# A hybrid mixer block on one core: the emission planner prices every operation, and TensorE keeps the planner's order

## The chip, the core and the metric

The kernel runs on one core of a Trainium2 chip. The core has TensorE (PE, matmuls into PSUM), VectorE (DVE), ScalarE (ACT), GpSimd (POOL) and SyncE (SP, which issues the DMAs here). Each engine runs its own instructions in the order in which they stand, and waits on semaphores for the others. The metric is the device time of one execution in microseconds (us); less is better.

## What is computed

One layer: RMS norm of x (2048 tokens by 1024), one input projection, four mixers of 256 channels each, one output projection, a second RMS norm and the residual.

```python
h = _rmsnorm(x, pre_norm_w[l])
proj = jnp.einsum('btd,de->bte', h, w_in[l])
p_gdn, p_rwkv, p_sc, p_gla = _split(proj, [GDN_COLS, RWKV_COLS, SC_COLS, GLA_COLS])
y_gdn = _gated_deltanet(p_gdn, ...)   # conv, chunks of 64, triangular solve per chunk, scan over chunks
y_rwkv = _rwkv7(p_rwkv, ...)          # token shift, decays, a recurrence over tokens (chunked in the kernel)
y_sc = _short_conv(p_sc, ...)
y_gla = _gla(p_gla, ...)              # gated linear attention, scan over chunks
out = jnp.einsum('bte,ed->btd', jnp.concatenate([y_gdn, y_rwkv, y_sc, y_gla], -1), w_out[l])
x = x + _rmsnorm(out, post_norm_w[l])
```

## The kernel before

**Tiling.** The tokens go in four blocks of 512. The projection of a block is made of large matmuls: 128 rows of weights by 512 tokens, in three passes (the high and low parts of the activations, tiles `hh` and `hl`, and of the weights, tiles `w`), into PSUM tile `pp`, of which there are two. A step of `proj` is four large matmuls (two where two tiles are woven), then a `yield`. The output projection at the end (tiles `woh`, `wol`) has the same form. In all there are 3808 large matmuls among 8180.

**Small work.** Per block and per pair of 128 tokens there is an inverse of eight unit-triangular matrices for the delta rule and again for RWKV (`inverse`: sixteen in all). A level of it is: `psi<-X,Bb` on TensorE, a VectorE multiply into `W` (line 591), `psi<-W,Yb` on TensorE, a VectorE add into `X` (line 596), a transpose and two copies into `Y` and `Yb`. The chains (`gdn_chain`, `rwkv_chain`, `gla`) carry the states `Sg`, `Sr`, `Sl` from chunk to chunk: for RWKV a loop is `psc<-Sr,AR` on TensorE, a ScalarE copy into `ru`, `psc<-ru,Yf`, a VectorE multiply into `UV`, `psc<-UV,BK`, and the addition to `Sr`. `gdn_prep`, `gdn_mats`, `gdn_more`, `rwkv_prep`, `rwkv_mats` and `rwkv_more` make what these need. Their matmuls and transposes go into `psa`, of which there are three tiles, each one PSUM bank; `psi` has one and `psc` two.

**What sets the order.** Each kind of work is a generator (a thread with a priority): chains 0, inverses 1, `prepare` 2, the outputs 3, statistics of the next block 4, loads of the output weights 5, and the large matmuls of `projections` 99. `weave` lets them take turns while the program is emitted. It keeps a running time `self.t`, to which only matmuls add (`mm`, `tr`); a thread that yields a number is ready again that much later, and the numbers are constants in `LAT` (for example 1.0 us from the matmul of an inverse's level to the next). The large matmuls go on until small work is ready and `BEAT` = 1.5 us have passed since the last. Then a list scheduler below the kernel takes the emitted program and orders each engine's instructions by its own estimate of what is ready, with the place of emission as priority; `high_priority` moves loads and evictions forward. So TensorE's order in the program is the scheduler's: of its instructions, 1946 stand behind one that was emitted later. A projection tile's group in `projections` waits for events, among them `("R", blk - 1)`: the RWKV tiles of a block may be overwritten when the block before has been put out.

Of the kernel before, what the change touches and what calls it, by code (L numbers as in the profile page):

```python
# [125 lines left out]
class Ring:  # L126
# [6 lines left out]
    def __call__(self):  # L133
# [15 lines left out]
    "lqk": (BL, 2), "lv": (BL, 2), "lkv": (384, 1), "lgz": (2 * BL, 1), "ld": (8, 1), "lg": (BL, 2), "n32": (32, 4), "gs": (TT, 2),  # L149
# [17 lines left out]
BEAT = 1.5  # L167
# [3 lines left out]
LAT = {"gates": 6.0, "ipre": 2.0, "gates2": 1.0, "norms": 3.2, "chan": 0.9, "pool": 1.38, "decay": 2.6, "mats": 2.2, "more": 1.4, "inv0": 1.0, "inv1": 2.2,  # L171
       "invr": 0.8, "chA": 1.0, "chB": 0.7, "chC": 0.48, "rpre": 5.0, "rchan": 4.5, "gpre": 3.0, "gA": 1.1,
       "gB": 0.62, "out": 8.0, "front": 0.3, "rdec": 0.6, "fdone": 2.0, "wo0": 2.8, "wo1": 1.4, "bonus": 2.5}
# [14 lines left out]
class K:  # L188
    def __init__(self, tc, a, out):
        self.tc, self.nc, self.a, self.out = tc, tc.nc, a, out  # L190
        self.t, self.left, self.ev, self.threads = 0.0, 0.0, {}, []


    def mm(self, out, w, x, **kw):
        n = math.prod(out.shape[1:])
        self.t += max(0.028, n * (1.67e-3 if w.dtype == F32 else 0.42e-3))
        return self.nc.tensor.matmul(out, w, x, **kw)  # L197

    def tr(self, out, x, ident):
        self.t += out.shape[1] * 0.83e-3  # L200
        return self.nc.tensor.transpose(out, x, ident)  # L201
# [5 lines left out]
    def done(self, *ev, lat=0.0):  # L207
        self.ev[ev] = self.t + lat
# [8 lines left out]
    def step(self, th):  # L217

        y = next(th[3], "end")
        if y == "end":  # L220
            self.threads.remove(th)
        elif isinstance(y, tuple):
            th[2] = y
        else:
            th[1] = self.t + y

    def weave(self):
# [3 lines left out]
        while self.threads:  # L231
# [10 lines left out]
            else:  # L242
                if not any(self.can(th) for th in self.threads):
                    w = [th[1] for th in self.threads if th[2] is None]
                    assert w, [(th[0], th[2]) for th in self.threads]
                    self.t = max(self.t, min(w))


    def setup(self, ctx):
# [16 lines left out]
        def bank(name, n):  # L266
            p = E(tc.tile_pool(name=name, bufs=n, space=PSUM))
            return lambda: p.tile([P, 512], F32, name=name, tag=name)
# [101 lines left out]
    def stats(self, blk, keep=None):  # L370
# [4 lines left out]
        ss, x, r = self.small(2 * TT), self.small(TT), self.R["gs"]()  # L375
# [29 lines left out]
    def front(self, blk, r):  # L405
# [3 lines left out]
        if blk:  # L409
            yield "bonus", blk - 1  # L410
        ps = self.psa()
# [9 lines left out]
        for k in range(KT):  # L421
# [12 lines left out]
            if k % 2:  # L434
                self.done("F", blk, k // 2, lat=LAT["fdone"])
            yield LAT["front"]
# [39 lines left out]
    def proj(self, blk, groups):  # L476
# [14 lines left out]
        for n, j, i, ks in work:  # L491
# [24 lines left out]
            if last:  # L516
                with self.tc.high_priority(offset=PRIO):
                    tiles[j][1](ps)
                if j + 1 == len(tiles) and after:
                    self.done("P", blk, after, lat=2.5)  # L520
# [37 lines left out]
    def inverse(self, Bh, Bl, n):  # L558
# [27 lines left out]
        yield LAT["ipre"]  # L586
        for lv in range(4):
# [4 lines left out]
            yield LAT["inv0"]  # L592
# [7 lines left out]
            yield LAT["inv0"] if lv == 3 else LAT["inv1"]  # L600
# [4 lines left out]
        yield LAT["inv0"]  # L605
# [13 lines left out]
        yield LAT["invr"]  # L619
# [8 lines left out]
        yield LAT["inv0"]  # L628
# [50 lines left out]
    def gates_prep(self):  # L679
# [31 lines left out]
        yield LAT["gates"]  # L711
# [16 lines left out]
        yield LAT["gates2"]  # L728

    def gdn_prep(self):  # L730
# [8 lines left out]
        for tt in range(TT):  # L739
# [11 lines left out]
            yield LAT["chan"]  # L751
# [16 lines left out]
        yield LAT["norms"]  # L768

    def gdn_mats(self, tt, Bh, Bl):  # L770
# [10 lines left out]
        yield LAT["pool"]  # L781
# [5 lines left out]
        yield LAT["decay"]  # L787
# [67 lines left out]
    def rwkv_prep(self, blk):  # L855
# [10 lines left out]
        for pr in range(2):  # L866
# [30 lines left out]
            yield LAT["rpre"]  # L897
# [18 lines left out]
        yield LAT["rchan"]  # L916

    def rwkv_bonus(self, blk):

        nc = self.nc  # L920
        for pr in range(2):
            v, gz, add = self.r["v"][pr], self.r["gz"][:, pr, :], self.r["add"][:, pr, :]
            self.split(*self.S, add)
            yield LAT["bonus"]
# [35 lines left out]
    def rwkv_more(self, tt, m):  # L960
# [8 lines left out]
        yield LAT["rdec"]  # L969
# [16 lines left out]
    def gdn_chain(self, tt, m, Y):  # L986
# [5 lines left out]
        for cp in range(2):  # L992
# [10 lines left out]
            yield LAT["chA"]  # L1003
# [6 lines left out]
            yield LAT["chB"]  # L1010
# [4 lines left out]
            if cp == 0:  # L1015
                yield LAT["chC"]
# [15 lines left out]
    def rwkv_chain(self, tt, m, Y):  # L1032
# [11 lines left out]
        for cp in range(2):  # L1044
# [6 lines left out]
            yield LAT["chB"]  # L1051
# [7 lines left out]
            yield LAT["chB"]  # L1059
# [4 lines left out]
            if cp == 0:  # L1064
                yield LAT["chC"]
# [58 lines left out]
    def prepare(self):  # L1124

        n = 0
        for blk in range(NBLK):
            for name in "GR":
# [8 lines left out]
                for pair in range(TT // 2):  # L1137
# [12 lines left out]
                    self.done("B", n, lat=LAT["mats"])  # L1150
# [4 lines left out]
                    self.done("M", n, lat=LAT["more"])  # L1155
# [3 lines left out]
            self.done("Lprep", blk, lat=LAT["gpre"])  # L1159

    def inverses(self):
        for n in range(NBLK * TT):
# [4 lines left out]
            self.done("I", n, lat=LAT["inv0"])  # L1167

    def chains(self):

        n = 0
        for blk in range(NBLK):
            for name, chain, norm, out in (("G", self.gdn_chain, self.gdn_norm, self.gdn_out),
                                           ("R", self.rwkv_chain, self.rwkv_norm, self.rwkv_out)):
                for tt in range(TT):
# [14 lines left out]
                    yield LAT["chC"]  # L1190
# [5 lines left out]
    def put(self, name, blk, tt, o, out):  # L1196
        if name == "R":
            yield "bonus", blk
        yield LAT["out"]
# [72 lines left out]
    def gla(self, blk, tt):  # L1272
# [15 lines left out]
        yield LAT["gA"]  # L1288
# [11 lines left out]
        for cp in range(2):  # L1300
# [4 lines left out]
            if cp == 0:  # L1305
                yield LAT["gB"]
# [7 lines left out]
        yield LAT["gB"]  # L1314
# [18 lines left out]
    def load_out(self):  # L1333
# [3 lines left out]
        for i in range(2):  # L1337
            for c in range(KT):
# [3 lines left out]
                yield LAT[f"wo{i}"]  # L1342
            self.done("W", i, lat=2.0)
# [114 lines left out]
```

## Time and profile before

| | us |
|---|---|
| three runs, median (lowest to highest) | 1389.66 (1388.5 to 1394.49) |
| the profiled execution, its own time | 1384.26 |
| its span, first to last instruction | 1382.4 |
| TensorE busy (9928 matmul records) | 1283.9, 93% |
| TensorE's weight loads busy | 976.0, 71% |
| VectorE busy | 955.6, 69% |
| ScalarE busy | 529.4, 38% |
| GpSimd busy | 355.0, 26% |

Busy times are shares of the span. A matmul's record is longer than the time until the next one starts, because matmuls are pipelined; so where the text prices TensorE it goes from start to start. A matmul of 32-bit floats has two records, a transpose or another type has one.

### The profile page before, as it was taken

The numbers are of one execution on the slowest core, as the hardware profiler recorded it, in microseconds if no ns is written. First come the engines' busy times: TensorE is split into PE (matmuls) and PEld (weight loads), VectorE is DVE, ScalarE is ACT, GpSimd is POOL, SyncE is SP. The second block draws the span as 40 slices with busy tenths as digits, with TensorE's granted clock in tenths as the row PEclk, the third lists the DMA queues.
The fourth block names the chain that finished last, engine by engine and source line by source line (L and its number), as shares of the span: only waits on it lengthen the run. The fifth ranks groups of instructions, "written<-read, shape, count | busy, mean of one in ns | idle before, by whom it ended". The sixth has DMA issues, their size and how long they took to land.

```text
span 1382.4 us, 25708 instructions
## 1 busy us (share of the span) xinstructions
PE 1283.9 (93%) x9928; PEld 976.0 (71%) x9928; DVE 955.6 (69%) x2194; ACT 529.4 (38%) x1181; POOL 355.0 (26%) x437
## 2 busy tenths in 40 slices
PE   5979878999989999999999898999998998999997
PEld 3757656777767667767777676677776766778886
DVE  5766798786765898777676996776769866533322
ACT  4653444333822441335523432345224333332221
POOL 5554343330120221111211211111211143333221
PEclk9999998999999999999999999999999999999999
DMA  7866442544534323354543333543444254334442
GB/s 269 278 230 229 164 171 92 176 147 165 176 112 152 117 97 125 112 183 142 167 155 129 116 104 111 173 144 112 145 141 134 83 170 138 111 104 145 146 151 99
DMA packets 98506, 204.47 MB, mean 148 GB/s; under 512 B 9152, under 2 KB 39248, under 8 KB 98384
## 3 DMA queue, kind: packets, MB, share of 16 engines
q1 hardware_dynamic: 98384, 202.83, 44.4%
q8 instruction: 78, 1.28, 0.4%
q14 instruction: 44, 0.36, 0.1%
HBM read 153.51 MB, written 49.28 MB: 147 GB/s over the span
## 4 chain that ended last, share of the span: by engine, by line
PE 52%; DVE 18%; issue 4%; POOL 3%; ACT 3%; DMA 2%; SPq 0%; POOLq 0%; ACTq 0%; DVEq 0%
PE pp L197 39%; PE psc L197 6%; PE psa L197 3%; PE psi L197 2%; PE psa L201 2%; POOL sm L354 2%; DVE Yb L583 1%; DMA x<-in_xt 1%; DVE X L596 1%; DVE W L591 1%; DVE Y L598 1%; DVE t L879 0%; DVE AR L895 0%; DVE M L949 0%; DVE og L1023 0%
## 5 line engine op out<-in xcount | busy, mean ns | idle before, releaser
L197 PE MATMUL pp<-hh,w 128*128 128x512 f32 (+1 forms) x2272 | 646.0, 408 | 5.3 <-DMA w<-parts 3.2
L197 PEld LDWEIGHTS pp<-hh,w 128*128 128x128 f32 (+1 forms) x2272 | 412.0, 190 | 90.6 <-DMA w<-parts 4.1
L197 PE MATMUL pp<-hl,w 128*128 128x512 f32 (+1 forms) x1152 | 342.7, 410 | 2.0 <-POOL hl L433 2.0
L197 PEld LDWEIGHTS pp<-hl,w 128*128 128x128 f32 (+1 forms) x1152 | 210.8, 191 | 47.7 <-POOL hl L433 3.8
L350 POOL TENSOR_TENSOR w<-raw,w 128x512 fp32r<-128x512 f32 (+1 forms) x102 | 129.4, 1270 | 218.0 <-ACT w L349 105.1
L349 ACT CAST w<-raw 128x512 fp32r<-128x512 f32 (+1 forms) x102 | 60.3, 593 | 141.9 <-issue 74.5
L354 POOL TENSOR_TENSOR sm<-sm,mhalf 128x4 f32<-128x4 f32 (+1 forms) x64 | 59.0, 922 | 209.2 <-DVE sm L1091 185.5
L659 DVE SCALAR_TENSOR_TENSOR pq<-pq,par,pq 128x512 f32<-128x512 f32 x72 | 59.1, 821 | 17.1 <-ACT pq L656 14.5
L197 PE MATMUL pp<-woh,w 128*128 128x512 f32 x256 | 69.5, 395 | 0.0
L197 PEld LDWEIGHTS <-Yb 128*128 128x128 f16 x640 | 26.0, 100 | 43.1 <-issue 18.8
L197 PE MATMUL psi<-W,Yb 128*128 128x64 f16 x640 | 33.6, 197 | 24.2 <-DVE W L591 20.8
L833 ACT COPY pq<-pp 128x512 f32<-128x512 f32 x36 | 21.1, 587 | 90.6 <-PE pp L197 90.6
L583 DVE COPY Yb<-Y 64x512 f16<-64x512 f16 x160 | 53.7, 336 | 2.1
L197 PEld LDWEIGHTS <-Bb 128*128 128x128 f16 x768 | 31.0, 99 | 33.8 <-issue 30.2
L197 PEld LDWEIGHTS pp<-woh,w 128*128 128x128 f32 x256 | 47.2, 188 | 9.5
L596 DVE TENSOR_TENSOR X<-psi,X 128x512 f16<-128x512 f32 x64 | 43.9, 686 | 13.3 <-PE psi L197 12.9
L197 PE MATMUL psi<-X,Bb 128*128 128x64 f16 x768 | 40.1, 197 | 12.9 <-DVE X L579 9.3
L591 DVE TENSOR_TENSOR W<-psi,c 128x512 f16<-128x512 f32 x64 | 44.0, 688 | 9.3 <-PE psi L197 8.3
L1391 DVE SCALAR_TENSOR_TENSOR pq<-pq,sm,x 128x512 f32<-128x512 f32 x32 | 25.1, 784 | 33.9 <-DMA x<-in_x 23.2
L598 DVE STREAM_TRANSPOSE Y<-X 128x512 f16<-128x512 f16 x64 | 45.1, 705 | 0.7
L1009 ACT COPY gu<-psc 64x128 f32<-64x128 f32 x64 | 16.6, 259 | 58.7 <-PE psc L197 57.4
L1380 ACT ACTIVATE x<-pp 128x512 f32<-128x512 f32 x32 | 19.1, 598 | 51.5 <-PE pp L197 51.5
(316 smaller groups left out, 2066.0 us busy)
## 6 DMA issues: line engine op xcount, KB each, us to landing
w<-parts SPq DMA_DIRECT2D x186, 512.0 KB, 3.3
parts<-w SPq DMA_DIRECT2D x62, 512.0 KB, 4.0
raw<-in_wt SPq DMA_DIRECT2D x62, 256.0 KB, 3.1
x<-in_x SPq DMA_DIRECT2D x56, 256.0 KB, 3.0
raw<-yd SPq DMA_DIRECT2D x32, 256.0 KB, 2.9
out<-pq SPq DMA_DIRECT2D x32, 256.0 KB, 2.3
x<-in_xt SPq DMA_DIRECT2D x24, 256.0 KB, 3.2
yd<-y SPq DMA_DIRECT2D x48, 128.0 KB, 2.5
```

Source lines behind the costliest of these rows:

```text
L197: return self.nc.tensor.matmul(out, w, x, **kw)
L201: return self.nc.tensor.transpose(out, x, ident)
L349: self.nc.scalar.copy(hi, src)
L350: self.nc.gpsimd.tensor_tensor(lo, src, hi.bitcast(F32), ALU.subtract)
L354: self.nc.gpsimd.tensor_tensor(dst, x, self.mhalf[:, 0:x.shape[1]], ALU.pow)
L583: nc.vector.tensor_copy(Yb[hs(c), :, hs(c)], Y[hs(c)])
L591: nc.vector.tensor_tensor(W, v(ps), m4(self.lev[lv]), ALU.mult)
L596: nc.vector.tensor_tensor(X2, v(ps), X, ALU.add)
L598: nc.vector.transpose(Y, X)
L659: nc.vector.scalar_tensor_tensor(acc, p[:, i:i + BL], self.pcol("conv", 4 * ct + i), acc, ALU.mult, ALU.add)
L833: nc.scalar.copy(p[:, 1:], ps)
L1391: nc.vector.scalar_tensor_tensor(o, o, r, x, ALU.mult, ALU.add)
```

## The change

The changed kernel emits the same arithmetic: the matmuls are the same 8180, the DMAs the same 556. What is new:

- `Chip`, `Engine` and `Clock` stand between the kernel and the engines. Every operation of VectorE, ScalarE and GpSimd and every DMA gets a price from its shape and a place in time: not before its tiles are written (or read, if it overwrites them), in the first free gap of its engine. `BY_ROW` tiles count by row.
- `pe` prices each matmul, with extra for going to large ones and for another tile shape, puts it not before its operands are written and its PSUM tile was read (`bank` hands over the time), and ties it behind the matmul emitted before it. So TensorE's order is the order of emission, without exception in all 8182 of its numbered instructions.
- The constants of `LAT` are gone. A thread yields a list of tiles and is ready when the clock says that they are written; `yield 0.0` stands where a step needs nothing.
- `BEAT` falls from 1.5 to 0.8 us; the statistics and the output norms get rings of their own (`ss`, `so`) instead of the shared `sm`.

The orders of VectorE, ScalarE, GpSimd and SyncE are still the list scheduler's.

```diff
+class Clock:
...
+    NS = {"vector": (0.155, 1.04e-3, 0.52e-3), "scalar": (0.17, 0.82e-3, 0.82e-3), "gpsimd": (0.12, 2.35e-3, 2.35e-3)}
...
+    def op(self, eng, name, ins, outs):
+        self.note(ins, outs, self.place(eng, max(self.now, self.there(ins, outs) + 0.07), self.cost(eng, name, ins, outs)))
...
     def mm(self, out, w, x, **kw):
-        n = math.prod(out.shape[1:])
-        self.t += max(0.028, n * (1.67e-3 if w.dtype == F32 else 0.42e-3))
-        return self.nc.tensor.matmul(out, w, x, **kw)
+        return self.pe(out, w, x, lambda: self.nc.tensor.matmul(out, w, x, **kw))
...
+    def pe(self, out, w, x, make):
+
+        side = lambda n: 32 if n <= 32 else 64 if n <= 64 else P
+        mode, n = (side(w.shape[0]), side(w.shape[-1] if w is not x else P)), math.prod(out.shape[1:])
+        big = n == BL and w.dtype == F32R
+        c = self.clock
+        change = 0.0
+        if big and not self.big:
+            change = 0.088 if self.mode == (P, P) else 0.22
+        elif mode != self.mode:
+            change = 0.09
+        self.mode, self.big = mode, big
+        t = max(self.t, max(c.there([w, x]), c.read.get(c.key(out), 0.0)) + 0.07)
+        self.stall += t - self.t
+        quarter = 1.0 if mode == (P, P) else 0.6 if max(mode) == P else 0.4
+        one = 0.227 if big else max(0.034, 0.036 + 0.5e-3 * n) * quarter if w.dtype == F32 else 0.030 + 0.2e-3 * n * quarter
+        self.t = t + change + one * (2 if w.dtype == F32 else 1)
+        c.now = self.t
+        c.note([w, x], [out], self.t + 0.17)
+        ins = make()
+        if self.prev is not None:
+            self.tc.add_manual_dep(ins.ins, self.prev.ins.name, mybir.DependencyInfo(mybir.DependencyClass.NoSync, mybir.DependencyReason.DATA), reason="the plan's order")
+        self.prev = ins
+        return ins
...
@@ -583,13 +708,13 @@
-        yield LAT["ipre"]
+        yield [X, Bb]
...
-            yield LAT["inv0"]
+            yield [W, Yb]
...
-            yield LAT["inv0"] if lv == 3 else LAT["inv1"]
+            yield [X]
...
@@ -748,7 +873,7 @@
-            yield LAT["chan"]
+            yield 0.0
...
@@ -1048,7 +1173,7 @@
-            yield LAT["chB"]
+            yield [D]
```

Three places of TensorE's order. In the rows, the number behind `x` counts like instructions in a row, and the numbers in names tell buffers apart.

The first is the first block's `gdn_prep`: sixteen transposes of the tiles `kq` into `psa`, four per tile of 128 tokens, behind the gate matmuls `psa<-gk`. Before:

```order
L197 MATMUL psa<-gk_92,bones 64x16 x2
L197 MATMUL pp<-hl,w_160 128x512 x4
L197 MATMUL pp<-hh,w_160 128x512 x4
L201 MATMUL psa<-cst,kq_181 128x128
L201 MATMUL psa<-cst,kq_182 128x128
L201 MATMUL psa<-cst,kq_181 128x128
L201 MATMUL psa<-cst,kq_182 128x128
L197 MATMUL pp<-hh,w_161 128x512 x4
L197 MATMUL pp<-hl,w_161 128x512 x4
```

Now:

```order
L284 MATMUL psa<-gk_92,bones 64x16 x2
L287 MATMUL psa<-cst,kq_185 128x128
L287 MATMUL psa<-cst,kq_186 128x128
L287 MATMUL psa<-cst,kq_185 128x128
L287 MATMUL psa<-cst,kq_186 128x128
L287 MATMUL psa<-cst,kq_185 128x128
L287 MATMUL psa<-cst,kq_186 128x128
```

All sixteen transposes now stand together, where eight large matmuls stood between each four.

The second is a level of the third block's second inverse, from the last `psi<-X,Bb` to the first `psi<-W,Yb`; VectorE makes `W` in between, and `rwkv_prep`'s work is in its queue. Before:

```order
L197 MATMUL psi<-X_149,Bb_152 128x64
L197 MATMUL psa<-S_163,bones 128x512
L197 MATMUL pp<-hh,w_161 128x512 x4
L197 MATMUL pp<-hh,w_159 128x512 x4
L197 MATMUL pp<-hl,w_159 128x512 x4
L197 MATMUL pp<-hh,w_159 128x512 x4
L197 MATMUL psc<-Sg,kq_181 128x128
L197 MATMUL psc<-Sg,kq_182 128x128
L197 MATMUL pp<-hh,w_160 128x512
L197 LDWEIGHTS Yb_153
L197 MATMUL psi<-W_148,Yb_153 128x64
```

Now:

```order
L287 MATMUL psa<-cst,t_90 128x128 x4
L284 MATMUL pp<-hh,w_165 128x512 x4
L284 MATMUL pp<-hl,w_165 128x512 x4
L284 MATMUL pp<-hh,w_165 128x512 x4
L284 MATMUL pp<-hh,w_163 128x512 x4
L284 MATMUL pp<-hl,w_163 128x512 x4
L284 MATMUL psa<-S_166,bones 128x512
L284 MATMUL psa<-S_167,bones 128x512
L284 MATMUL pp<-hh,w_163 128x512 x4
L284 MATMUL pp<-hh,w_164 128x512 x4
L284 LDWEIGHTS Yb_157
L284 MATMUL psi<-W_152,Yb_157 128x64
```

There were 17 large matmuls in this gap, and there are 28; none stands alone any more.

The third is the end of the first block's RWKV chain, while TensorE works on the second block's projection. Before:

```order
L197 MATMUL psc<-Sr,AR_63 128x128
L197 MATMUL psc<-Sr,AR_64 128x128
L197 MATMUL pp<-hh,w_161 128x512 x4
L197 MATMUL pp<-hh,w_159 128x512 x4
L197 MATMUL psc<-ru_80,Yf_87 64x64 x4
L197 MATMUL pp<-hl,w_159 128x512 x4
L197 MATMUL pp<-hh,w_159 128x512 x4
L197 MATMUL pp<-hh,w_160 128x512
L197 MATMUL psc<-UV_79,BK_65 64x64 x2
L197 MATMUL psc<-UV_79,BK_66 64x64 x2
```

Now:

```order
L284 MATMUL psc<-Sr,AR_63 128x128
L284 MATMUL psc<-Sr,AR_64 128x128
L284 MATMUL psc<-ru_80,Yf_87 64x64 x4
L284 MATMUL psa<-t_202,cst 128x256
L284 MATMUL psc<-UV_78,BK_65 64x64 x2
L284 MATMUL psc<-UV_78,BK_66 64x64 x2
L284 MATMUL psc<-UV_78,M_76 64x64 x2
L284 MATMUL psc<-UV_78,M_77 64x64 x2
```

Between the links of the chain stood large matmuls; now 166 small ones follow each other here without a large one, because the second block's RWKV tiles wait for `("R", 0)`.

## Rows read from the trace of the kernel before

**Rows 1.** The page's head and busy times, and the granted TensorE clock over the span.
```profile
span 1382.4 us, 25708 instructions
PE 1283.9 (93%) x9928; PEld 976.0 (71%) x9928; DVE 955.6 (69%) x2194; ACT 529.4 (38%) x1181; POOL 355.0 (26%) x437
core 0: 1382.4 us, clock 0.985
```

**Rows 2.** Stretches: from:to, length, busy us (instructions) of PE, PEld, DVE, ACT, POOL, PEclk, DMA.
```profile
0.00:12.00 12.00, 0.00 (x0) 0.00 (x0) 4.26 (x24) 5.19 (x12) 4.57 (x11) 1.00 0.85 292
...
730.00:830.00 100.00, 93.09 (x787) 70.41 (x785) 89.86 (x208) 37.69 (x84) 16.34 (x21) 1.00 0.36 118
```

**Rows 3.** TensorE's waits: who waited for whom, us in total, times, longest.
```profile
PE psi L197 <- DVE W L591: 20.8, 18, 2.9
PE psa L201 <- POOL gs L354: 12.1, 1, 12.1
PE psi L197 <- DVE X L579: 9.3, 7, 1.9
PE psc L197 <- DVE gu L999: 6.3, 8, 2.3
```

**Rows 4.** TensorE around 292 us, in order of time: start, length, operation, idle before.
```profile
290.46 1.08 PE L197 MATMUL pp<-hh,w 128*128 128x512 f32 x4
291.47 0.45 PE L197 MATMUL psc<-UV,BK 128*64 128x64 f32 x8
291.75 0.64 PE L197 MATMUL psc<-UV,M 128*64 128x64 f32 x16
292.32 0.41 PE L197 MATMUL psi<-W,Yb 128*128 128x64 f16 x8
292.56 0.71 PE L197 MATMUL pp<-hl,w 128*128 128x512 f32 x2
293.11 1.09 PE L197 MATMUL pp<-hh,w 128*128 128x512 f32 x4
294.04 0.62 PE L197 MATMUL pp<-hl,w 128*128 128x512 f32 x2
```

**Rows 5.** After a wait near 187 us: a stretch as in rows 2, and TensorE's rows.
```profile
186.70:190.10 3.40, 3.15 (x22) 2.44 (x23) 3.20 (x8) 1.49 (x3) 0.00 (x0) 0.50 0.90 306
...
186.95 0.61 PE L197 MATMUL psi<-W,Yb 128*128 128x64 f16 x8 [2.52 <-DVE W L591]
...
187.95 1.48 PE L197 MATMUL pp<-hl,w 128*128 128x512 f32 x3
189.23 0.65 PE L197 MATMUL psi<-X,Bb 128*128 128x64 f16 x8
```

**Rows 6.** The first `gdn_prep`, around 60 and 68 us, in order of time.
```profile
60.43 1.28 ACT L721 ACT_TABLE_LOAD   x1
60.55 0.60 PE L201 MATMUL psa<-cst,kq 128*128 128x128 f32 x4
60.91 1.17 PE L197 MATMUL pp<-hh,w 128*128 128x512 f32 x4
...
67.96 0.74 ACT L748 COPY kT<-psa 64x256 f32<-64x256 f32 x2
68.73 0.60 ACT L746 ACTIVATE t<-psa 128x512 f32<-128x512 f32 x1
```

**Rows 7.** One loop of the RWKV chain and the norm behind it, in order of time.
```profile
1183.30 0.61 PE L197 MATMUL psc<-Sr,AR 128*128 128x128 f32 x4
...
1187.04 0.58 DVE L1030 TENSOR_TENSOR Sr<-Sr,psc 64x128 f32<-64x128 f32 x2 [1.39 <-PE psc L197]
1187.37 0.74 ACT L1071 COPY or<-psc 64x256 f32<-64x256 f32 x2 [0.99 <-PE psc L197]
...
1192.17 0.43 DVE L1095 TENSOR_TENSOR or<-or,sm 128x256 f32<-128x256 f32 x1 [0.81 <-POOL sm L354]
```

**Rows 8.** A VectorE group of the page: shapes, count, busy, mean ns, idle before.
```profile
L591 DVE TENSOR_TENSOR W<-psi,c 128x512 f16<-128x512 f32 x64 | 44.0, 688 | 9.3 <-PE psi L197 8.3
```

More of the change, by code (lines that the diff above doesn't have):

```diff
@@ new lines, with __init__, __getattr__, call @@
+class Engine:
+    def __init__(self, clock, name, eng):
+        self.clock, self.name, self.eng = clock, name, eng
+    def __getattr__(self, op):
+        f = getattr(self.eng, op)
+        def call(*a, **kw):
+            isap = lambda x: hasattr(x, "shape") and hasattr(x, "dtype")
+            outs = [x for x in (kw.get("out", None if "out" in kw else a[0] if a else None), kw.get("accum_out")) if isap(x)]
+            ins = [x for x in list(a[0 if "out" in kw else 1:]) + [v for k, v in kw.items() if k not in ("out", "accum_out")] if isap(x)]
+            if op == "dma_start":
+                self.clock.dma(ins, outs)
+            else:
+                self.clock.op(self.name, op, ins, outs)
+            return f(*a, **kw)
+        return call
@@ L176, in h4, with __init__ @@
+class Chip:
+    def __init__(self, nc):
+        self.clock, self.nc = Clock(), nc
+        self.vector, self.scalar, self.gpsimd, self.sync = (Engine(self.clock, n, getattr(nc, n)) for n in ("vector", "scalar", "gpsimd", "sync"))
+        self.tensor = nc.tensor
 def h4(t):
@@ L223, in step @@
             th[2] = y
+        elif isinstance(y, list):
+            th[1] = self.clock.there(y) + 0.07
         else:
@@ L246, in weave @@
                     self.t = max(self.t, min(w))
+                    self.clock.now = self.t
     def setup(self, ctx):
@@ L267, in bank, with take @@
             p = E(tc.tile_pool(name=name, bufs=n, space=PSUM))
-            return lambda: p.tile([P, 512], F32, name=name, tag=name)
+            held = [None] * n
+            def take():
+                t = p.tile([P, 512], F32, name=name, tag=name)
+                old = held.pop(0)
+                held.append(t)
+                if old is not None:
+                    self.clock.note([t], [], self.clock.there([], [old]))
+                return t
+            return take
         self.pp, self.psa, self.psi, self.psc = (bank(n, k) for n, k in BANKS.items())
@@ L516, in proj @@
             if last:
+                self.clock.last = 0.0
                 with self.tc.high_priority(offset=PRIO):
@@ L1198, in put @@
             yield "bonus", blk
-        yield LAT["out"]
+        yield [o]
         out(blk, tt, o)
```

132 lines of the change are left out of this document (89 added, 43 removed).

## Prediction

> **What bounds the kernel now.** I read the busy shares first, then TensorE's waits, then single stretches in order of time. TensorE is busy 1283.9 of 1382.4 us [rows 1], and no other engine comes near. It does nothing in the first 12 us, where it waits for the first statistics (the wait of 12.1 us on `gs`) [rows 2, 3]. So the kernel is bound by TensorE, and there are three things to gain: the waits in the middle, what TensorE pays for going back and forth between large and small matmuls, and the time at half clock.
>
> The waits are mostly the inverses': 20.8 us for `W` in 18 waits and 9.3 us for the first `X` of an inverse [rows 3]; the chains add 6.3 us for `gu` and smaller ones. They are not spread evenly. In the stretch from 730 to 830 us VectorE is busy 89.9 of 100 us and TensorE only 93.1 [rows 2]: there `rwkv_prep`'s wide operations stand in the same queue as the inverse's `W` and `X`. The order was made by a scheduler that believed `W` would be there. The wait of 2.52 us near 187 us [rows 5] is one of those.
>
> Going back and forth: a plain group of four large matmuls goes from 293.11 to 294.04, 0.23 us each. The four before `psc<-UV,BK` take 290.46 to 291.47, 1.01 us, that is 0.08 more; the two behind `psi<-W,Yb` take 292.56 to 293.11, 0.55 us, that is 0.09 more [rows 4]. A visit to small work costs 0.17 us beside its own matmuls.
>
> The clock: it was 0.985 over the span [rows 1], and since it stands at 1.2 or 2.4 GHz, about 3% of the span, 41 us, went at half. After the wait of 2.52 us it was 0.50 for 3.4 us, and three large matmuls took from 187.95 to 189.23, 0.43 us each, against 0.23 [rows 4, 5]. If all 41 us were large matmuls this would cost 19 us.
>
> **The change, part by part.** The sum is made against the profiled execution, 1384.3 us; the median of the runs, 1389.7, lies 0.4% higher, and the result is scaled by that.
>
> *Fewer visits.* Counted in the two orders, 438 stretches of small matmuls become 397. 41 x 0.17 = 7 us less. The shape of TensorE's tile changes 649 times before and 616 times now; 33 of these at 0.09, as an estimate, give 3 us more. I take -10, with ends at -4 (only half of a visit's price goes) and -16. Page TensorEngine Tiling (Array Packing) of the Trainium skill, section Key Properties, says that changing the tiling mode, not just the tile, drains TensorE. By that rule alone only the 33 changes of shape would count, and this part would be -3. The rows differ: `psi<-W,Yb` and the large matmuls behind it have the same 128 by 128 tile, and the 0.09 us is there [rows 4].
>
> *The inverses' waits.* The new plan puts a price on VectorE's operations: 0.155 + 512 x 0.00104 = 0.687 us for `W`, and the trace has 0.688 [rows 8]. So its queue of VectorE is about the real one, where the constants in `LAT` knew nothing of a queue. The order shows it: from the first to the last level of each block's second inverse, where `rwkv_prep` is in the queue, 98, 95, 101 and 95 large matmuls stand in between before, and 112, 104, 152 and 164 now. In the third and fourth block that is 51 and 69 more, 12 and 16 us of other work at 0.23; in the first two it is only 14 and 9 more, 2 to 3 us. I take -16 of the 20.8 us on `W` and -8 of the 9.3 on `X`: -24, with ends at -8 (the first two blocks stay as they are and the rest is halved) and -30 (all gone).
>
> *The chains' waits.* Steps are now ready when their tiles are written, which brings chain matmuls nearer to what they wait for; the prices are better, the distances shorter. I take 0, with ends at -6 (all of `gu`) and +6 (as much again).
>
> *Stalls that the held order brings in.* The list scheduler moved large matmuls in front of small ones that were not ready; now nothing moves. A step that needs a `psa` bank which is still being read makes TensorE wait, with everything behind it: the large matmuls, and the chains behind them. In `gdn_prep` all sixteen transposes stand together and there are three banks. The third group needs the bank of the gate matmuls, which ScalarE reads only after its table load (1.28 us); the fourth needs the first group's bank, which takes a square of 0.60 and copies of 0.74 more: 2.6 us [rows 6]. TensorE has three groups of transposes for that time, 60.55 to 60.91 each, 1.1 us [rows 6]. That leaves 1.5 us per block, 6 in all, or 1 where the table is there already. `rwkv_mats` and `gdn_mats` for two tiles in a row have the same trouble once a block each; a second one waits for one VectorE eviction of the size in [rows 8], 0.69 us: 8 x 0.69 = 5, with ends at 0 (the bank is free by then) and 11 (two evictions). Together +11, ends +1 and +19.
>
> *One long hole.* At the end of the first block's RWKV chain 166 matmuls (278 records) now follow each other without a large one. At 0.035 us a record (`psc<-UV,M`: 16 records from 291.75 to 292.32) [rows 4] that is 10 us of work. What has to happen in that time is three loops of the chain, 1183.30 to 1187.62, 4.3 us each, and the norm, 1187.37 to 1192.60, 5.2 us [rows 7]: 17.5 us without the last addition. So TensorE stands 7 us; +7, with ends at +3 (loops whose matmuls find TensorE free are shorter) and +12 (VectorE also has the second block's inverse to do).
>
> *Clock.* Fewer waits of 2 us and more, so fewer stretches at half clock; but the long hole may start one. -5, ends -12 and +4.
>
> *The rest at nothing.* 556 DMAs and all arithmetic are the same; a half tile of weights still gives twelve large matmuls, 2.8 us, of cover for the next load. The rings `ss` and `so` take away a reuse of small tiles that no row of the waits names. The first 12 us and the end, an unbroken run of large matmuls, stay.
>
> Sum: -10 - 24 + 0 + 11 + 7 - 5 = -21. 1384.3 - 21 = 1363.3, times 1.0039 is 1368. All good ends together give -65, all bad ones +25: 1325 and 1415.
>
> **The rivals.** *The stalls hardly show* (faster by much): the plan counted them and the visits cost more than I think. Ends -16, -30, -12, with +2 for the banks and +3 for the hole: -53, 1336. For it: the prices fit. Against: the sixteen transposes stand there in the order.
>
> *VectorE is the bound where the waits are* (no change): 89.9 of 100 us [rows 2] leaves no room, so a wait that is filled comes back at the next level, and the inverses' -24 becomes -5: sum -2, 1388. Against it: the third and fourth block's inverses have been given 12 to 16 us more. The Trainium skill, page Perfetto Trace Analysis, section Identifying the Most-Contended Engine, would say so too: it judges TensorE's headroom by its weight loads, here 71%, and VectorE by its busy share. By that rule VectorE's 90% binds in such a stretch. The trace agrees only there; over the span VectorE has 69% [rows 1].
>
> *VectorE goes another way than the plan* (slower): only TensorE is held to the plan, while VectorE's order is still the list scheduler's. Each time it puts one 512-wide operation ahead of one on which TensorE's plan counts, TensorE stands 0.69 us [rows 8], with the large matmuls behind it. The inverses alone have 16 x 11 = 176 such steps. At 30 of them, one in six, the gain of 21 is gone; at 60 the kernel takes +20, 1410. For it: nothing ties VectorE to the plan. Against: its order follows emission with TensorE's fixed, and moves are not all bad.
>
> That the change doesn't do what it says is out for TensorE: its order is the order of emission throughout.
>
> **How the numbers follow.** My forecast, 1350 to 1383, has 0.45. The strong gain (below 1350) has 0.20, no change 0.17, slower 0.18. The predicted time is 1368. Half of the strong gain lies below 1335 and half of the slower case above 1403: that is the range. A measurement of this kernel can tell about 0.5% from no change. Faster by over that has 0.45 + 0.20 = 0.65; within it 0.17; slower 0.18.
>
> **What would show it.** Right: TensorE's waits on `W` under 6 us; new waits on `psa` for `kT` and `sx` in each block's `gdn_prep`; one stretch between 310 and 340 us where TensorE is busy little more than half of some 18 us. Wrong: if the waits on `W` are still 20 us, the plan's VectorE isn't the chip's. If waits on `psa` are over 20 us, the banks were underpriced. If the waits are small and the time is unchanged, the price of a visit is wrong.

## The result and the profile after

The changed kernel takes 1439.02 us (median; 1432.38 to 1445.55), the kernel before 1389.08 on the same chips. The ratio is 1.0354, with a 95% interval of 1.0297 to 1.0411. It is slower by 50 us, where 1368 was forecast; the time lies outside the range.

The profiled execution took 1438.88 us, 54.6 more than that of before. The page's head and busy times and the granted clock, which answer to [rows 1]:

```profile
span 1437.1 us, 25744 instructions
PE 1304.9 (91%) x9928; PEld 991.6 (69%) x9928; DVE 971.3 (68%) x2194; ACT 533.7 (37%) x1183; POOL 353.2 (25%) x437
core 0: 1437.1 us, clock 0.953
```

No engine has more to do. TensorE's busy time is 21 us longer with the same instructions, and its clock fell from 0.985 to 0.953. VectorE's busy time is 15.7 us longer with the same 2194 operations; why was not measured. Its waits answer to [rows 3] (line 284 has the matmuls now, 287 the transposes, 253 every other operation):

```profile
PE psa L287 <- DVE or L253: 12.4, 6, 3.8
...
PE psc L284 <- DVE Sr L253: 9.5, 7, 2.9
PE psi L284 <- DVE X L253: 9.5, 8, 3.0
PE psa L284 <- DVE M L253: 8.4, 4, 3.2
PE psa L287 <- DVE og L253: 8.1, 6, 3.2
PE psa L287 <- DVE attn L253: 7.1, 4, 3.6
...
PE psc L284 <- DVE UV L253: 6.1, 4, 4.0
PE psa L287 <- ACT kT L253: 4.9, 1, 4.9
PE psa L284 <- DVE attn L253: 4.5, 3, 1.8
...
PE psi L284 <- DVE W L253: 1.8, 4, 0.9
```

The rows of this view add up to 124 us, against 90 before. What the plan was made for has come: `W` went from 20.8 us to 1.8. But all other waits together grew by 53 us. 49 of these are on seven tiles: outputs that are put (`or`, `og`), states and results of the chains (`Sr`, `UV`), and tiles that VectorE or ScalarE makes out of a bank of `psa` which TensorE wants next (`M`, `attn`, `kT`).

Then the clock. The trace has 10 stretches at half clock before and 24 after. These are the sums over them, first all instructions and then those with `pp` alone (the large matmuls); the first two lines are of before, the last two of after. The columns are the length and the busy times:

```profile
sum 44.07, PE 37.12 PEld 29.58 DVE 29.73 ACT 13.41 POOL 6.12; mean PE 3.71 PEld 2.96 DVE 2.97 ACT 1.34 POOL 0.61
sum 44.07, PE 25.75 PEld 17.13 DVE 0.00 ACT 1.17; mean PE 2.58 PEld 1.71 DVE 0.00 ACT 0.12
```

```profile
sum 138.43, PE 116.33 PEld 87.41 DVE 100.44 ACT 47.10 POOL 32.39; mean PE 4.85 PEld 3.64 DVE 4.18 ACT 1.96 POOL 1.35
sum 138.43, PE 62.98 PEld 44.87 DVE 0.00 ACT 3.23; mean PE 2.62 PEld 1.87 DVE 0.00 ACT 0.13
```

94 us more go at half clock: 37 us of large matmuls (62.98 - 25.75) and 42 us of small ones (53.35 - 11.37), the rest idle. Waits of 2 us and more are 17, where there were 6. And TensorE is longer without large matmuls: from one large matmul to the next it is more than 6 us at 14 places (135 us in all), where it was at 5 (39 us).

One place shows how both come about. TensorE of the changed kernel around 295 us, in order of time (start, length, operation, idle before):

```profile
294.28 0.60 PE L287 MATMUL psa<-cst,BK 128*128 128x128 f32 x4
294.71 0.38 PE L287 MATMUL psa<-cst,rv 128*128 128x128 f32 x2
299.11 0.70 PE L284 MATMUL psc<-UV,BK 128*64 128x64 f32 x8 [4.02 <-DVE UV L253]
299.74 0.69 PE L287 MATMUL psa<-cst,or 128*128 128x128 f32 x2
300.08 1.20 PE L284 MATMUL pp<-hh,w 128*128 128x512 f32 x2
301.08 1.05 PE L284 MATMUL pp<-hl,w 128*128 128x512 f32 x2
301.94 1.91 PE L284 MATMUL pp<-hh,w 128*128 128x512 f32 x4
```

And the same link of the chain in the kernel `loose-big` (below), where large matmuls may pass:

```profile
294.40 0.38 PE L287 MATMUL psa<-cst,rv 128*128 128x128 f32 x2
294.54 0.71 PE L284 MATMUL pp<-hh,w 128*128 128x512 f32 x2
295.08 0.62 PE L284 MATMUL pp<-hl,w 128*128 128x512 f32 x2
295.54 1.07 PE L284 MATMUL pp<-hh,w 128*128 128x512 f32 x4
296.45 0.61 PE L284 MATMUL pp<-hl,w 128*128 128x512 f32 x2
296.90 0.61 PE L284 MATMUL pp<-hh,w 128*128 128x512 f32 x2
297.80 0.45 PE L284 MATMUL pp<-hh,w 128*64 128x512 f32 x1 [0.28 <-ACT pq L253]
298.17 0.45 PE L284 MATMUL psc<-UV,BK 128*64 128x64 f32 x8
```

`UV` is late by about the same in both. In the changed kernel TensorE stands 4.02 us in front of it and the clock is then at half: the two large matmuls from 300.08 to 301.08 take 0.50 us each. In the other kernel thirteen large matmuls fill the time and the clock stays at 1.00 from 290 to 304 us.

### The profile page after: what moved, and what is told of

Its sections match the earlier page's. It is cut to its first block, busy times and chain, and to the rows that moved or that the text cites. A ratio compares the mean times of both kernels' runs of the same rounds, so it can differ in the third digit from the quotient of the medians.

```text
span 1437.1 us, 25744 instructions
## 1 busy us (share of the span) xinstructions
PE 1304.9 (91%) x9928; PEld 991.6 (69%) x9928; DVE 971.3 (68%) x2194; ACT 533.7 (37%) x1183; POOL 353.2 (25%) x437
## 4 chain that ended last, share of the span: by engine, by line
PE 62%; DVE 20%; issue 6%; ACT 4%; POOL 4%; DMA 3%; SPq 0%; POOLq 0%; ACTq 0%; DVEq 0%
PE pp L284 46%; PE psc L284 7%; PE psa L284 4%; PE psi L284 3%; PE psa L287 3%; POOL sm L253 2%; DVE pq L253 2%; DVE n L253 2%; DVE t L253 1%; DVE sm L253 1%; DMA x<-in_x 1%; DMA w<-parts 1%; DVE Y L253 1%; ACT t L253 1%; DVE radd L253 1%
## 5 line engine op out<-in xcount | busy, mean ns | idle before, releaser
L284 PEld LDWEIGHTS pp<-hh,w 128*128 128x128 f32 (+1 forms) x2272 | 418.5, 193 | 99.5 <-DMA w<-parts 4.9
L253 POOL TENSOR_TENSOR sm<-sm,mhalf 128x4 f32<-128x4 f32 x48 | 49.6, 1034 | 196.1 <-DVE sm L253 196.1
L253 DVE SCALAR_TENSOR_TENSOR pq<-pq,par,pq 128x512 f32<-128x512 f32 x100 | 79.5, 795 | 23.0 <-ACT pq L253 20.8
L253 DVE TENSOR_TENSOR X<-psi,X 128x512 f16<-128x512 f32 x80 | 55.0, 688 | 39.2 <-PE psi L284 38.8
L253 ACT COPY pq<-pp 128x512 f32<-128x512 f32 x68 | 39.8, 585 | 111.9 <-PE pp L284 111.7
L253 DVE TENSOR_TENSOR W<-psi,c 128x512 f16<-128x512 f32 x80 | 54.9, 686 | 14.4 <-PE psi L284 12.9
L253 DVE SCALAR_TENSOR_TENSOR pq<-pq,so,x 128x512 f32<-128x512 f32 x32 | 25.4, 793 | 33.4 <-DMA x<-in_x 23.0
L253 ACT ACTIVATE pq<-pq 128x512 f32<-128x512 f32 (+1 forms) x36 | 22.7, 632 | 53.7 <-DVE pq L253 53.6
L253 ACT ACTIVATE pq<-pp,dpar 128x512 f32<-128x512 f32 x52 | 35.9, 691 | 12.9 <-PE pp L284 12.8
```

Source lines behind the costliest of these rows:

```text
L253: return f(*a, **kw)
L284: return self.pe(out, w, x, lambda: self.nc.tensor.matmul(out, w, x, **kw))
```

## Experiments: what the held order costs

Each kernel was timed against the kernel before on its own chip, and ratios are to that, with 95% intervals.

**The tie left out** (`free`):

```diff
-        if self.prev is not None:
+        if False:
```

> The changed kernel with one thing undone: the tie between each matmul and the one emitted before it is left out, so the list scheduler orders TensorE again; the plan, its prices and the lists of tiles stay. Theory A (the held order costs: TensorE stands behind a small matmul that is not ready, where the scheduler would have put large ones first): the waits fall back from some 128 us in all to 90 or less, the clock comes back to 0.98, and the time is 1375 to 1400. Theory B (the plan itself is at fault: its steps are called ready too early and the small work comes in too dense): the time stays at 1425 or more. In between: both.

Measured: 1379.59 us, ratio 0.9960 (0.9936 to 0.9983), clock 0.981, waits of 82 us in all. All of the loss is gone, and 0.4% of a gain is left. Theory A is right, B is out.

**Only the large matmuls left out of the tie** (`loose-big`):

```diff
+        if big:
+            return ins
         if self.prev is not None:
```

> The changed kernel, but the large matmuls are left out of the tie: the small ones keep the order of emission among themselves, and the list scheduler places the large ones between them. Theory A1 (what costs is that a large matmul may not pass a small one that waits): most of the 59 us between the changed kernel and the one without ties comes back, 1380 to 1400, clock 0.97 or more. Theory A2 (what costs is the order among small matmuls: a psa step that waits for its bank keeps the chains behind it): 1415 or more.

Measured: 1375.77 us, 0.9919 (0.9892 to 0.9947), clock 0.979. A1, and 4 us better than its range: the order among the small matmuls costs nothing that shows; that a large one may not pass costs all of it, 1.0354 - 0.9919, some 60 us. From one large matmul to the next it is more than 6 us at 2 places only, 7.2 us at the most, though the plan is the same.

**Only matmuls into `psa` left out** (`loose-psa`):

```diff
+        if out.tensor.name.startswith("psa") if hasattr(out, "tensor") else out.name.startswith("psa"):
+            return ins
         if self.prev is not None:
```

> The changed kernel, but matmuls and transposes into psa are left out of the tie; psi, psc and large ones keep the order of emission. Theory E (the stalls are those of psa: banks that are still read, and outputs or, og, lu and attn that are not written, about 60 of the 130 us of waits): 1400 or less. Theory A1 (any small matmul that is not ready holds up the large ones, the chains' and the inverses' as well): about half, 1405 to 1425.

Measured: 1408.89 us, 1.0164 (1.0107 to 1.0222), clock 0.964: as A1 says. The `psa` steps are some 26 of the 60 us, chains and inverses the rest.

**The tie without the plan**: the kernel before, with each matmul tied behind the one emitted before it (`tied-old`).

```diff
     def mm(self, out, w, x, **kw):
...
-        return self.nc.tensor.matmul(out, w, x, **kw)
+        return self.tie(self.nc.tensor.matmul(out, w, x, **kw))
```

> The kernel before with one thing added: each matmul is tied behind the one emitted before it; the old constants stay and decide when a step is ready. Theory A (the held order costs by itself): slower than before by 30 us or more, 1420 or above, with waits on W and on chain results that are longer than the 20.8 and 6.3 us of before. Theory B (only the new plan is at fault): within 10 us of 1389.

Measured: 1429.52 us, 1.0342 (1.0297 to 1.0387): theory A. The old constants, held to, fail at `W` and `gu`, where the kernel before had its longest waits too; the new plan, held to, fails elsewhere. TensorE's waits of `tied-old`:

```profile
PE psi L197 <- DVE W L599: 40.5, 22, 5.5
PE psc L197 <- DVE gu L1007: 23.9, 21, 4.8
```

**VectorE tied to its order of emission too** (`held-ve`):

```diff
-            return f(*a, **kw)
+            ins = f(*a, **kw)
+            if self.name == "vector":
+                if self.prev is not None:
...
+                self.prev = ins
+            return ins
```

> The changed kernel with VectorE's instructions tied in the order of their emission too (before this, 1745 of them stand behind one that was emitted later, with this none). The rival of the prediction (VectorE goes another way than the plan, and TensorE, which is held to it, stands for that): faster than the changed kernel by 20 us or more, 1419 or less. If the stalls are not VectorE's order: 1430 to 1450, or slower still, because an operation that is not ready now holds up VectorE too.

Measured: 1660.39 us, 1.1977 (1.1922 to 1.2032). The rival of the prediction, that TensorE waits because VectorE leaves the plan, is not borne out in this form: a VectorE held to its order of emission is far worse. Its page and two of TensorE's waits:

```profile
PE 1359.2 (82%) x9928; PEld 1030.4 (62%) x9928; DVE 982.4 (59%) x2194; ACT 535.5 (32%) x1181; POOL 342.9 (21%) x437
...
PE psi L291 <- DVE X L254: 64.6, 31, 6.5
PE psi L291 <- DVE W L254: 61.1, 22, 8.7
```

It is not the order that the plan had in mind, which fills gaps; that one was not tried, so the rival itself stays untested. Tying VectorE also delayed the first statistics (a wait of 30 us on `gs`, against 12.4).

## Experiments: what makes the new waits, with the tie kept

**The old distances given back** (`spaced`), behind the gates, between the transposes of `gdn_prep`, behind its norm, behind two steps of the mixers' matrices, and before an output is put:

```diff
-        yield 0.0
+        yield 1.0
...
-            yield 0.0
+            yield 0.9
...
-        yield 0.0
+        yield 3.2
...
-        yield 0.0
+        yield 1.4
...
-        yield [o]
+        yield 8.0
```

> The changed kernel, tie kept, but the steps that the change made ready at once get the old distances back: 1.0 us behind the gates, 0.9 between the four groups of transposes of gdn_prep, 3.2 behind its norm, 1.4 behind the steps of rwkv_more and gdn_mats, and 8.0 before an output is put. Theory I (banks of psa and outputs that are asked for at once make the new waits: or, og, lu, kT, sx, attn and M, 45 us): 1415 or less. Theory A1 (whatever waits holds up the large matmuls; with other distances other steps wait): 1425 to 1445.

Measured: 1409.84 us, 1.0162 (1.0130 to 1.0194). Theory I has the time; the waits show what it is worth:

```profile
PE psi L284 <- DVE X L253: 15.3, 12, 3.1
...
PE psi L284 <- DVE W L253: 10.9, 10, 3.2
PE psa L284 <- DVE t L253: 8.2, 3, 5.4
...
PE psa L287 <- DVE or L253: 2.2, 3, 1.3
```

`or` is down from 12.4 to 2.2 and `og` is no longer among the large ones, but `X`, `W` and `t` come up. Steps called ready at once are about half of the loss.

**A margin on every list of tiles** (`margin`):

```diff
-            th[1] = self.clock.there(y) + 0.07
+            th[1] = self.clock.there(y) + 0.8
```

> The changed kernel with one number changed: a step that waits for a list of tiles is called ready 0.80 us after the clock's time, not 0.07. Theory D (VectorE's and ScalarE's real order runs later than the plan's by one operation or two, and TensorE stands for it): the waits on or, og, lu, Sr, UV and X, some 60 us, fall to half or less, the clock rises above 0.97, and the time is 1405 or less. If the waits are banks of psa and stretches without a large matmul, on which the list has no say, 1425 to 1445.

Measured: 1436.33 us, 1.0371 (1.0342 to 1.0401), clock 0.947. No gain; the waits on `or` grew to 27.3 us. Theory D, as one delay for all lists, is out while the tie stands.

**BEAT back at 1.5** (`beat15`):

```diff
-BEAT = 0.8
+BEAT = 1.5
```

> The changed kernel with BEAT back at 1.5 us, all else as changed. Theory C (small work is let in too often, and its results are asked for too soon): at least half of the loss comes back, 1415 or less, and TensorE's waits fall by 20 us or more. Theories A and B, where the density of small work is set by what is ready and by steps that follow each other without a large matmul: within 10 us of 1439.

Measured: 1428.76 us, 1.0313 (1.0279 to 1.0347). 6 to 10 us at the most; not theory C.

**DMAs priced lower in the plan** (`loads`):

```diff
-        self.note(ins, outs, self.place("dma", max(self.now, self.there(ins, outs)), size * 3.4e-6) + 2.0)
+        self.note(ins, outs, self.place("dma", max(self.now, self.there(ins, outs)), size * 1.0e-6) + 1.0)
```

> The changed kernel with another price for DMAs in the plan, 1.0 us and 1.0e-6 us a byte where it has 2.0 and 3.4e-6. Theory F (the plan lets large matmuls wait for weights more than the 7.1 us that the trace shows, takes small work for ready in that time, and TensorE comes to it too early): TensorE's waits fall by 15 us or more, 1425 or less. If the plan's price of loads does not matter: within 8 us of 1439.

Measured: 1431.43 us, 1.0333 (1.0284 to 1.0382). Not told apart from the changed kernel; the price doesn't matter.

## Experiments: what the half clock costs by itself

The longest stretch at half clock is where no large matmul is to be had, at the end of the first block's RWKV chain. Large matmuls of a constant, whose results are overwritten, were added there, and at a few such places elsewhere: three at a place (`hot`), then one (`warm1`) and two (`warm2`).

```diff
+                main = self.threads[-1] if self.threads else [0]
+                if name in ("psc", "psi") and main[0] == 99 and not self.can(main):
+                    for _ in range(3):
+                        self.mm(t.rearrange(...), self.bones_r, self.bones_r.unsqueeze(1).to_broadcast([P, 4, P]), start=True, stop=True)
                 return t
```

> The changed kernel with something added: wherever a psc or psi tile is taken while no large matmul may be emitted, three independent 128x512 matmuls of a constant are put into that tile before its own (36 in all, 30 of them in the stretch around 375 to 406 us, that is 7 us there at 0.23 us each); their results are overwritten. Theory G (the half clock of that stretch costs time by itself): the clock stays at full from 379 to 400 us, the stretch takes no longer than its 31 us, and the time is 1425 to 1439. Theory H (the stretch is bound by the chain's way through VectorE and ScalarE, and the clock only accompanies it): 1440 to 1450, with the stretch longer by 3 to 7 us.

> As hot, with one independent large matmul at each place instead of three, some 3 us in the stretch. If its clock is at full and the half clock had cost 6 us there (theory G): the stretch takes 28 to 30 us against 31.9 of the changed kernel, and the time is 1434 to 1438. If the chain's path sets the length (theory H): 31.5 to 33 us. If the clock is at half again, this run says nothing on the price, and the stretch takes 32 to 35 us.

> As hot, with two independent large matmuls at each place, some 6 us in the stretch. Theory G: 30 to 31.5 us for the stretch at full clock. Theory H: 31.5 to 33 us, as with three.

The stretch from 375 to 406 us, columns as in [rows 2], of the changed kernel, of `warm1`, `warm2` and `hot`; the third value from the end is the granted clock:

```profile
375.00:406.00 31.00, 22.67 (x272) 16.55 (x267) 24.44 (x74) 8.34 (x22) 7.33 (x10) 0.67 0.07 23
```

```profile
375.00:406.00 31.00, 23.67 (x291) 16.18 (x291) 24.84 (x76) 8.99 (x24) 7.33 (x10) 0.89 0.08 27
```

```profile
375.00:406.00 31.00, 23.88 (x306) 15.78 (x302) 25.79 (x80) 9.21 (x24) 8.55 (x12) 1.00 0.08 27
```

```profile
375.00:406.00 31.00, 25.31 (x316) 17.50 (x316) 25.13 (x77) 8.55 (x22) 8.54 (x11) 1.00 0.08 25
```

Its first and last instruction in the changed kernel and in `warm2`:

```profile
374.67 0.45 PE L284 MATMUL psc<-UV,BK 128*64 128x64 f32 x8
...
406.55 1.18 PE L284 MATMUL pp<-hh,w 128*128 128x512 f32 x4
```

```profile
374.63 0.45 PE L284 MATMUL psc<-UV,BK 128*64 128x64 f32 x8
...
404.67 1.18 PE L284 MATMUL pp<-hh,w 128*128 128x512 f32 x4
```

From that first to that last instruction it takes 31.88 us in the changed kernel, 30.58 in `warm1` (10 matmuls added), 30.04 in `warm2` (20) and 32.56 in `hot` (33). With 20 x 0.23 = 4.6 us of work added, at full clock, it is 1.8 us shorter. So the half clock costs between 1.8 and 6.4 us there, for 16 us of small matmuls that ran in it: theory G, though for less than the 8 us that the small matmuls would save by their own length. This rests on one trace of each kernel. TensorE's order in `warm1` and `warm2` is that of the changed kernel, but for the added matmuls and two transposes that come earlier; a few of VectorE's operations changed places too, and their share in the 1.8 us was not measured. `warm1` lies between the lengths that its theories gave, with the clock at half for a part. Where the rest of the 8 us went wasn't measured; the chain's way through VectorE and ScalarE would hide it, whose operations take the same in the changed kernel and in `warm2` (`W` 0.69 us, `ru` 0.36). `hot` fits neither theory: its stretch is 0.7 us longer, at full clock. It has levels of the inverse in another order and 16 more small records in the stretch, so it can't be compared. The kernels' times are 1439.02 (ratio 1.0365, 1.0340 to 1.0389), 1439.28 (1.0389, 1.0354 to 1.0423) and 1435.69 us (1.0348, 1.0318 to 1.0378): 2 us can't be told at that size.

## Experiments: a version that beats both

With the large matmuls left out of the tie, as in `loose-big`, the other knobs were tried again, with the edits of `beat15`, `margin` and `loads` on top of it.

**The old constants with only the small matmuls tied** (`old-big`), in the kernel before:

```diff
-        return self.nc.tensor.matmul(out, w, x, **kw)
+        ins = self.nc.tensor.matmul(out, w, x, **kw)
+        return ins if n == BL and w.dtype == F32R else self.tie(ins)
```

> The kernel before, with its old constants, and only the small matmuls tied to each other in the order of their emission; the large ones are free. It asks whether the order among small matmuls or the new plan brings the gain of 10 us that the changed kernel shows with its large matmuls free. If the small matmuls' order is enough: 1372 to 1380. If the new plan is needed: 1385 or more, since the old constants know nothing of VectorE's queue.

Measured: 1377.62 us, 0.9939 (0.9924 to 0.9954), against 0.9919 with the new plan. So the order among small matmuls alone gives 0.6%, the plan alone (`free`) 0.4%, both 0.8%; the intervals overlap, and which of the two brings more isn't shown. The gain of `old-big` is not in the waits, which add up to 99 us against 90 before: TensorE's busy time is 15.5 us shorter.

**BEAT at 1.5** (`big-beat`):

> The changed kernel with the large matmuls left out of the tie, and BEAT back at 1.5 us. It asks whether the shorter beat is worth anything once large matmuls may pass. If small work that is let in more often costs visits (0.17 us each by the kernel before): 1365 to 1373, under the 1375.8 of the same kernel with a BEAT of 0.8. If the list scheduler decides anyway: 1373 to 1379. If the earlier emission feeds VectorE better: 1380 or more.

Measured: 1370.06 us, 0.9879 (0.9847 to 0.9912): where it was expected if small work let in more often costs visits, though the interval overlaps that of `loose-big`.

**A margin of 0.5** (`big-margin`):

```diff
-            th[1] = self.clock.there(y) + 0.07
+            th[1] = self.clock.there(y) + 0.5
```

> The changed kernel with the large matmuls left out of the tie, and a step called ready 0.50 us after the clock's time, not 0.07. If the waits that are left (W 9.5, og 9.6, M 6.3, or 5.4 us) come from steps called ready too early: 1360 to 1372. If they come from banks and from VectorE's queue: 1373 to 1385.

Measured: 1363.42 us, 0.9841 (0.9814 to 0.9868). A margin, which at 0.8 us was worth nothing under the tie, is worth 0.8% here. The time is as expected, the reason isn't shown: the waits fell by 5 us only (87 to 82), those on `W` and `og` by 10.5 while `M` and `or` rose by 8, and TensorE's busy time fell by 10.7.

**DMAs priced lower** (`big-loads`):

> The changed kernel with the large matmuls left out of the tie, and DMAs priced in the plan at 1.0 us and 1.0e-6 us a byte. If the plan's price of loads puts small work too early (the 8 us that this price was worth in the tied kernel): 1366 to 1372. If the scheduler's freedom with the large matmuls already gives this back: 1373 to 1379.

Measured: 1374.31 us, 0.9922 (0.9893 to 0.9950): nothing.

**Margin of 0.5 and BEAT of 1.5** (`best`):

> The changed kernel with large matmuls left out of the tie, a margin of 0.50 us and a BEAT of 1.5. If the 12 us of the margin and the 6 us of the beat add up: 1357 or less. If both take away the same waits: 1360 to 1370.

Measured: 1357.28 us, 0.9782 (0.9757 to 0.9808): 2.2% faster than before, and the two add up. Of the 26 us by which its span is shorter than that of before, 19 are TensorE's busy time (1283.9 to 1264.7) and the rest waits. It has 398 stretches of small matmuls, where the kernel before has 438, and inside the span 34 us at half clock against 42. By the prediction's price of a visit and with half of the 8 us these make some 11 of the 19 us, as an estimate; where the other 8 come from was not measured. Its page:

```profile
span 1356.1 us, 25718 instructions
PE 1264.7 (93%) x9928; PEld 964.6 (71%) x9928; DVE 973.0 (72%) x2194; ACT 533.5 (39%) x1183; POOL 352.3 (26%) x437
```

**Margin of 1.0, BEAT of 0.8** (`best2`):

> The changed kernel with large matmuls left out of the tie, a margin of 1.0 us and a BEAT of 0.8. If steps called ready too early still make most of the waits that the margin of 0.50 left: 1350 to 1360. If 0.50 was enough: 1360 to 1370; if the chains now start too late, 1370 or more.

Measured: 1368.11 us, 0.9861 (0.9835 to 0.9887): 0.5 was enough.

## Why the prediction was wrong, step by step

*The inverses' waits, -24.* Right. `W` and the first `X` were 30.1 us [rows 3] and are 4.6: 1.8 for `W`, and of the 9.5 on `X` 2.8 for the first `X` of an inverse (two waits, at 308 and 392 us). So -25.5; the waits on the later `X` rose from 3.5 to 6.7. The rival of a bound VectorE had only -5 here, and is out. In the stretch of [rows 2] from 730 to 830 us TensorE is now busy for more of the time and VectorE for less. A part of that is other work, since the third block's `M` is now made from 821 us on, and was from 790; but from 760 to 860 us VectorE is busy 82.3 us and TensorE 96.4:

```profile
730.00:830.00 100.00, 96.80 (x702) 74.61 (x700) 75.67 (x169) 37.05 (x76) 17.05 (x30) 0.98 0.43 144
```

*The long hole, +7.* Right in size by luck. The stretch that was meant, with its 278 records, lies at 375 to 406 us, not 310 to 340, and TensorE is idle there for 8.3 of 31 us. I had 10 us of work in 17.5 us. It was 22.67 us of work, most of it at half clock, in 31, and the two errors cancel. Nor is it one hole, but the longest of the 14 places without a large matmul.

*Stalls that the held order brings in, +11.* **This step failed.** The held order's stalls measure +44 where I took +11, with an end at +19. Of its two places `gdn_prep` came out near its sum, but not as priced: `kT` and `sx` wait 7.1 us, against 1.4 before, so +6. That is 2.0 us in the first block and 5.1 in the third, none in the others, where I had 1.5 in each. The wait in the third block's `gdn_prep`:

```profile
669.50 0.66 PE L287 MATMUL psa<-cst,kq 128*128 128x128 f32 x4 [0.26 <-ACT sx L253]
675.01 1.11 PE L287 MATMUL psa<-cst,kq 128*128 128x128 f32 x4 [4.86 <-ACT kT L253]
```

But the banks of `rwkv_mats` and `gdn_mats` (`M`, `attn`) went from 5 to 20 us, +15 where I took +5: I priced one eviction of 0.69 us and left out what stands in front of it in VectorE's queue: for the 2.79 us before 821.97 TensorE waits for `M`, and VectorE makes parts of `n`, `Y` and `Yb` until it turns to `M` at 821.23. By the prediction's own sign (waits on `psa` over 20 us) the banks were underpriced: `M`, `attn`, `kT` and `sx` make 27. The outputs `or`, `og` and `lu` went from 4 to 23 us and were not in the sum at all; nor were 4 us on weights. I looked for stalls at places that caught the eye in the order, where I should have priced each of the instructions that the scheduler had moved. That was in the text: 1946 of them stood behind a later one. Every small matmul that isn't ready keeps all large ones behind it, and `loose-big` puts the sum of that, clock included, at some 60 us. The Trainium skill, page PSUM — Partial Sum Buffer, section Engine vs sequencer instructions, says that matmuls start and complete in program order. The trace agrees: at 299.11 nothing passes for 4.02 us. The prediction had this mechanism (TensorE waits, "with everything behind it") and counted too few places for it.

*The chains' waits, 0.* Too low: `gu` fell from 7.8 to 3.6 us, but `Sr`, `UV` and `ru` rose by 14, so +10, beyond the end of +6.

*Clock, -5.* **This failed too**, and in sign. I tied the half clock to waits of 2 us and more and expected fewer of them. There are more, 17 against 6, and the long hole is at half as well, though TensorE waits 2 us or more only once in it. What that costs, as an estimate: of the 37 us more of large matmuls at half, 0.20 in 0.43, since one takes 0.43 us and not 0.23 [rows 4, 5]: 17 us. Of the 42 us more of small ones, by the price of the stretch above (1.8 to 6.4 us for 16 us), 5 to 17. Together 22 to 34 us. The Trainium skill, page TensorE: Matmul & The Clock Gate, section Terms, prices throttled time at the time by one minus the ratio of the clocks; by that rule, as an estimate, 94 us at half would cost 47. The runs show less; 15 of the 94 us are waiting.

*Fewer visits, -10.* Not contradicted, not shown. The stretches of small matmuls are 397, as counted. The waits' +34 and the clock's +22 to +34 make 56 to 68; the trace has +54.6. What is left for the visits and the rest is -1 to -13. `loose-big` has as many stretches as before (436) and is faster than the changed kernel, so the visits don't make the loss. The kernels that have fewer with the large matmuls free, `old-big` (403) and `best` (398), have 15.5 and 19.2 us less of TensorE's busy time than before, and `loose-big` 2.3 less; that speaks for a price, but the time at half clock differs as well.

*The ends.* The good ends of the parts add up to -60 and the bad ones to +29, not -65 and +25 as the prediction has it; the bad end is then 1419, and the measured time is still beyond it.

*The rivals.* The slower one gave 1410, nearest of all, but no run here tests its mechanism, that VectorE goes another way than the plan; `held-ve` tied VectorE to a third order. Its sentence that TensorE stands with the large matmuls behind it is what happens. I gave it a price of one VectorE operation at a time, 0.69 us; behind the first statistics, 16 waits of 2 to 5 us make 50 of the 111 us.

What stays open: how the 60 us divide between waits and clock more closely than above, since each brings the other; whether VectorE's departures from the plan make the late operands, and whether a VectorE held to the plan's own order would help.

## What to carry to other kernels

An engine that runs in order needs independent work between a step and its result; a plan that fixes the order is hostage to its worst estimates, because every late operand stops all that stands behind it. Fix the order among the small, dependent operations if it helps, and leave the large independent ones free to be placed where the real waits are: here that turned +3.5% into -0.8%, and with a margin and a longer beat into -2.2%. When a change takes a scheduler's freedom away, price what the scheduler had moved, not the places that look bad.

## What the runs showed of the hardware

TensorE stayed at half clock from 379.09 to 399.57 us although it was busy 16.00 of these 20.48 us and waited at most 2.13 us at a time. In the kernel before it was at half for 6.82 us from 1074 us with TensorE busy all the time by the records. So in these two stretches the clock can't be read off the busy time. With twenty independent large matmuls among the small ones it was at full in the first of them (1.00 in `warm2`), and by its one trace they cost less than they gave back, 30.04 us against 31.88.
